# A decoder layer on one core: another order of the five products of a feed-forward chunk, and three smaller edits behind it

## The chip, the core and the metric

The kernel runs on one core of a Trainium2 chip. Five engines work side by side, each through its own list of instructions in order: TensorE (PE in the profile; PEld is its weight load), VectorE (DVE), ScalarE (ACT), GpSimd (POOL) and SyncE (SP), which here only issues DMAs. They wait for each other through semaphores. The metric is the time of one execution in microseconds (us).

## What is computed

One layer over 1056 tokens (1024 of a prompt, 8 x 4 being decoded), width 1024, inner width 2816. The part that matters is the feed-forward block and the embedding step behind it; the mixing step ahead of them is untouched.

```python
f = _rms(x, n_ffn_pre)
f = (jax.nn.silu(f @ w_gate) * (f @ w_up)) @ w_down
x = x + _rms(f, n_ffn_post)
x = x + jax.nn.sigmoid(x @ w_ple_gate) * (p @ w_ple)
```

All of it is float32. The kernel makes a float32 product out of three faster ones: every operand is split into a high part (a cast on ScalarE, L185) and a low part (the difference on VectorE, L186), and the product of the two low parts is left out.

## The kernel before

**Products with seven multiplications.** The three large matrix products of this part are done as 2 x 2 block products with seven block multiplications in place of eight. Their operands are sums and differences of blocks, named S1 to S4 for the weights and T1 to T4 for the tokens, beside plain blocks B11 to B22. A multiplication is named after the weights it uses: P1, P2 and P4 use plain weights, S1 to S4 sums.

**The channel chunks.** Gate and up projection go through 22 chunks `c` of 128 inner columns (`chunk(c)`). P1 and P2 of all chunks are made earlier by `ahead`, and their results are parked in device memory. `part_load` (L1159) fetches them as a tile `p` that holds p1 and c11. What is left for a chunk are five products on TensorE: P4, S2, S4, S3, S1 (P4 reads the weight tile `w`, the S products read `sh` and `sl`; the tokens are `fh`). A product is 24 matmuls of 128 x 264 into one PSUM pair (two banks, `b` in the profile); there are four pairs. VectorE empties a pair with a sum (`add`, L1127): p1 += S2, then u4 = p1 + S4, u3 = p1 + S3, c21 = u3 + P4, and S1 (p5 in the code) is added to u3 and u4. The chunk ends with c21 times silu(c11), silu of u4 on ScalarE (L1202), u3 times u4, and in `chunk_put` (L1069 and L1064) the differences t1, t2, t4 and the one for T3, which go to device memory as the operands `xd` of the down projection. One chunk of each two stores five such tiles, the other two.

**Weights of the chunks.** `need` walks a list of items. For each chunk the list has `half` (the weights of P4, one tile `w`, cast from a quarter of the raw up weights) and `sums` (GpSimd makes the four sums in place over the raw tiles `wr` and `a`, L1099, and then four tiles `sh`, `sl` are split from them). GpSimd's first sum overwrites what `w` is split from, so it comes after that split. All split weights share one ring of 2 x W_PAIRS = 8 tiles: five for a chunk, so the weights of two chunks on take tiles that products of the current chunk free.

**The down projection** follows the chunks: five groups of columns for each of P1, P2, S2, S3, P4, S1, S4, with four pairs filled in turn (`down`), and the tokens `xo` loaded from `xd` (L1323) and split. Its weight sums are made during the chunks by GpSimd: `down_sums`, eleven slabs of four operations `ds` (L1303), each slab loaded by SyncE and stored to `dd`. During the first part of the down stage `gate_sums` makes the sums for the embedding gate (`ws`, L1099; loads L1267, stores to `gd` L1277), one step at every call of `gates_on`.

**The last stage** multiplies by w_ple_gate: eight half products with W1, then S4, S1, S2, S3 and P4 with W2, each followed by `ple_end` (sigmoid, L1483, times the embedding product `pp`, plus the residual `xm`, then the store of the output). The two embedding weights WE are taken from the ring of eight and stay in use until the end; `need(..., 3)` prepares the weights three items ahead. The norm between (`rstd_steps`, with a tile `hl`, and then `o`, `x` and `eh` rows) runs on VectorE and ScalarE at the same time.

**What sets the order.** The program is written in one order, and a scheduler places the instructions of each engine from it; instructions marked with `keep_in_program_order` stay where they are. At run time nothing is reordered on VectorE, ScalarE, GpSimd or SyncE: an instruction that waits holds all that stands behind it.

Of the kernel before, what the change touches and what calls it, by code (L numbers as in the profile page):

```python
# [12 lines left out]
AF = mybir.ActivationFunctionType  # L13
ALU = mybir.AluOpType
# [22 lines left out]
FFC = 22  # L37
# [3 lines left out]
QN = T // 4  # L41
# [28 lines left out]
def trunk_kernel(  # L70
# [68 lines left out]
    def pair():  # L139
        return psum[0].tile([P, 2, 512], F32, tag="p", name=nm("b"))  # L140
# [7 lines left out]
    def row(s="r"):  # L148
        return tmp(HN, s).rearrange("p (i n) -> p i n", n=QN)
# [61 lines left out]
    def w_split(j, home=None):  # L211
        if j >= len(plan) or j in pairs:
            return
        w_load(j)
        shape = plan[j][1]
        hi, lo = (home(shape, F32R) if home else w_tile(shape, s) for s in ("wh", "wl"))
        split(hi, lo, raws[j])
        pairs[j] = (hi, lo)
# [37 lines left out]
    WG = []  # L256
# [51 lines left out]
    def need(k, ahead=LOOK):  # L308

        for i in range(len(made), max(k + 1, min(k + ahead + 1, until[0]))):  # L310
            kind, js = ITEMS[i]
            if kind == "loaded":
                made[i] = w_tile([P, 2, 512], "wf")
                queue(nc.sync.dma_start(made[i].bitcast(F32), js[0]))
                continue
            for j in plans(kind, js):
                w_load(j)
            if kind == "direct":
                w_split(js[0])
                made[i] = pairs[js[0]]  # L320
            elif kind == "half":
                t = w_tile([P, KC, P], "w2")
                made[i] = t[:, 0:4, :], t[:, 4:8, :]
                split(*made[i], raws[js[0]][:, js[1] : js[1] + 4, :])
            else:
                made[i] = w_sums(*(raws[j] for j in js))
            for kind, js in ITEMS[i + 1 : i + 3]:
                for j in plans(kind, js):
                    w_load(j)
        return made[k]  # L330
# [707 lines left out]
    def operand(key, i=None):  # L1038
        while (key not in fx) if i is None else ((key, i) not in ready):
            step(chains[0])  # L1040
        return fx[key]
# [24 lines left out]
    def chunk_put(c, h0, h1):  # L1066

        def sub(out, a, b):
            ve.tensor_tensor(out, a, b, op=ALU.subtract)  # L1069

        pair_, slot = c // SLAB, c % SLAB
        if slot == 0:
            stage("B11", pair_, h0)
            t1 = row("t1")
            sub(t1, h1, h0)
            stage("T1", pair_, t1)
            evens[:] = t1, h1
            return
        t1, b12 = evens
        stage("B21", pair_, h0)  # L1080
        stage("B22", pair_, h1)
        t2, t4 = row("t2"), row("t4")
        sub(t2, h1, t1)
        stage("T2", pair_, t2)
        sub(t4, h0, t2)
        stage("T4", pair_, t4)
        sub(b12, h1, b12)
        stage("T3", pair_, b12)
# [23 lines left out]
    def ops4(w, x, i):  # L1112

        at = [(k // 2, 2 * (k % 2) + i) for k in range(4)]
        return [
            (w[0][:, k, :], w[1][:, k, :], x[0][t][:, j, :], x[1][t][:, j, :]) for k, (t, j) in enumerate(at)
        ]

    def product(w, x, onto=None):

        ps = pair()[:, :, :QN] if onto is None else onto
        for i in range(2):
            gemm(ps[:, i, :], ops4(w, x, i), onto=onto is not None)
        return ps

    def add(out, a, b, op=ALU.add):
        ve.tensor_tensor(out, a, b, op=op)  # L1127
# [28 lines left out]
    def part_load(c):  # L1156
        if c < FFC:
            parts[c] = act_tile([P, 2, 2, QN], s="p")
            nc.sync.dma_start(parts[c], p_d[c])  # L1159

    def seven(w, sums, p1, x):

        p4 = product(need(w), x("T4"))
        s = need(sums)
        add(p1, p1, product(s["S2"], x("T2")))
        u4 = row("u4")
        add(u4, p1, product(s["S4"], x("B22")))
        u3 = row("u3")
        add(u3, p1, product(s["S3"], x("T3")))
        c21 = row("c21")  # L1170
        add(c21, u3, p4)
        yield c21
        p5 = product(s["S1"], x("T1"))
        add(u3, u3, p5)
        yield u3
        add(u4, u4, p5)
        yield u4

    sums = []

    def sums_on(n=1):
        if not sums:
            sums.append(down_sums())
        for _ in range(n):
            next(sums[0], None)

    def chunk(c):

        part_load(c + 1)
        p = parts.pop(c)  # L1190
        p1, c11 = p[:, 0], p[:, 1]
        ins = se.activation(c11, c11, AF.Silu)
        if c == 0:
            tc.keep_in_program_order(ins)
        made7 = seven(*WG[c], p1, operand)
        c21 = next(made7)
        add(c21, c21, c11, ALU.mult)
        sums_on()
        c22 = next(made7)
        c12 = next(made7)  # L1200
        sums_on(1 + c % 2)
        se.activation(c12, c12, AF.Silu)  # L1202
        add(c22, c22, c12, ALU.mult)
        chunk_put(c, c21, c22)
        if c == FFC - 2:
            sums_on(4 * NSLAB)

    os_ = [[None] * 2 for _ in range(2)]
    x2 = [[None] * 2 for _ in range(2)]
# [166 lines left out]

    share[0] = 0.5
    queued[:] = [None]
    gates = (x for n in range(4) for x in gate_sums(n))

    def gates_on(e, j):
        if j == 3:
            next(gates, None)

    def squares_end(o, b):
# [88 lines left out]
    def ple_end(gate, xm, pp, m, b, pieces=WHOLE, onto=None):  # L1474

        sg = row("sg")
        for at in pieces:
            at = (slice(None), *at)
            g = gate[at]
            if onto is not None:  # L1480
                add(onto[at], onto[at], g)
                g = onto[at]
            se.activation(sg[at], g, AF.Sigmoid)  # L1483
        for at in pieces:
            at = (slice(None), *at)
            add(sg[at], sg[at], pp[at], ALU.mult)
            add(sg[at], sg[at], xm[at])
            dst = by_row(y_o[:, m, HN * b : HN * (b + 1)])
            nc.sync.dma_start(dst[at], sg[at])
# [62 lines left out]
    on()  # L1552
    u2 = {}
    for a, _ in PAIRS:
        ps = product(need(W1[a][0], 3), e7["B11"])
        if a in (5, 1):
            both = two_rows("p1")
        u2[a] = both[a in (7, 3)]
        se.copy(u2[a], ps)
        xm = x2_row(a, 0)  # L1560
        pp = embed(WE[a // 4], a, 0)
        on()
        product(need(W1[a][1], 3), e7["B21"], ps)
        ple_end(ps, xm, pp, a, 0)
        on()

    c12, p5 = {}, {}
    for k in LATE:
        for g in range(2):
            for i in range(2):  # L1570
                a, b = PAIRS[2 * g + i]
                w = need(W2[k, a], 3)
                if k != "P4":
                    w = [w[:, h].rearrange("p (k n) -> p k n", n=P) for h in range(2)]
                last = k == LATE[-1] and g == i == 1
                key = {"S4": "B22", "P4": "T4"}.get(k, "T" + k[1])
                ps = product(w, e7[key])
                if k == "S4":
                    if i == 0:
                        both = two_rows("c12")  # L1580
                    c12[a] = both[i]
                    se.copy(c12[a], ps)
                elif k == "S1":
                    if i == 0:
                        both = two_rows("p5")
                    p5[a] = both[i]
                    se.copy(p5[a], ps)
                    add(c12[a], c12[a], ps)
                elif k == "S2":
                    xm = x2_row(a, 1)  # L1590
                    pp = embed(WE[a // 4], a, 1)
                    add(u2[a], u2[a], ps)
                    ple_end(u2[a], xm, pp, a, 1, onto=c12[a])
                elif k == "S3":
                    xm = x2_row(b, 1)
                    pp = embed(WE[b // 4], b, 1)
                    add(u2[a], u2[a], ps)
                    ple_end(u2[a], xm, pp, b, 1, onto=p5[a])
                else:
                    xm = x2_row(b, 0)  # L1600
                    if last:
                        pp = late_pp
                    else:
                        pp = embed(WE[b // 4], b, 0)
                    if g == 1 and i == 0:
                        late_pp = embed(WE[PAIRS[3][1] // 4], PAIRS[3][1], 0)
                    ple_end(ps, xm, pp, b, 0, onto=u2[a], pieces=PIECES if last else WHOLE)
                on()
# [90 lines left out]
```

## Time and profile before

| what | us |
|---|---|
| three runs of the kernel before | 1070.43, 1070.84, 1075.89 |
| median | 1070.84 |
| the profiled execution | 1073.98 |
| its span in the profile | 1072.2 |
| channel chunks, about | 395 to 728 |
| down projection, about | 728 to 958 |
| last stage, about | 958 to 1072 |

The span is the time from the first to the last instruction of the profiled execution; the time of the execution is 1.8 us longer. Rows of the profile name an instruction by its line in the kernel, the tiles it writes and reads (`u<-p,b`), their shapes and how often it occurs. In a group of instructions the first number behind the bar is the busy time in us and the second the mean of one in ns; behind the next bar stands the idle time of the engine ahead of them and what ended it. A busy time near 100% of TensorE says that it had work, not that it ran at full speed; the granted clock is a column of its own.

### The profile page before, as it was taken

To read this page: it belongs to the slowest core of one execution; us is meant where nothing else is said; L and a number is where in the kernel's file an instruction comes from. 1 tells how busy PE (TensorE), PEld (TensorE's weight loads), DVE (VectorE), ACT (ScalarE), POOL (GpSimd) and SP (SyncE) were. 2 spreads that over 40 slices of the span, in tenths; PEclk is the share of its full clock that TensorE was granted. 3 is DMA by queue.
4 is the path that set the end of the run, shared out by engine and by line. 5 is a ranking of instruction groups with operands and counts; after the bars stand their busy time and mean duration, and the time that the engine had idled before them with its cause. 6 is when DMAs were issued, how large, how long until landed. Compare 5 with 4: busy or idle time off the path is not lost.

```text
span 1072.2 us, 20467 instructions
## 1 busy us (share of the span) xinstructions
PE 1046.4 (98%) x8175; PEld 1028.4 (96%) x8175; DVE 774.9 (72%) x1078; ACT 472.7 (44%) x872; POOL 272.7 (25%) x213
## 2 busy tenths in 40 slices
PE   9999999999999999899999999998999999999997
PEld 8999988899999999899999999998999999999997
DVE  6866378977798827769768787786457667979765
ACT  7522277765677642221222222332454445444421
POOL 1045023200000038567566654312022200000000
PEclk9999999999999999999999999999999999999999
DMA  8121311362889757877777775457687887747763
GB/s 300 60 73 40 101 57 41 124 230 80 285 294 316 245 204 249 298 273 256 248 274 264 260 249 192 144 182 245 199 288 249 318 269 243 229 166 254 230 231 117
DMA packets 115903, 224.56 MB, mean 209 GB/s; under 512 B 9668, under 2 KB 60132, under 8 KB 115808
## 3 DMA queue, kind: packets, MB, share of 16 engines
q1 hardware_dynamic: 114480, 221.49, 61.4%
q10 hardware_dynamic: 1328, 1.77, 0.5%
q8 instruction: 64, 1.05, 0.4%
q14 instruction: 31, 0.25, 0.1%
HBM read 156.15 MB, written 67.07 MB: 208 GB/s over the span
## 4 chain that ended last, share of the span: by engine, by line
PE 42%; POOL 4%; DVE 4%; issue 4%; DMA 3%; ACT 1%; SPq 0%; POOLq 0%; DVEq 0%; ACTq 0%
PE b L135 42%; POOL ds L1303 2%; POOL wr L1099 1%; POOL a L1099 1%; DMA p<-pd 1%; DVE u L1127 1%; DMA wr<-in_w_dn_dram 0%; DVE w L186 0%; DMA xo<-xd 0%; DMA xd<-u 0%; DVE t L1069 0%; DVE o L1251 0%; DVE x L1127 0%; DVE sg L1127 0%; DMA dd<-ds 0%
## 5 line engine op out<-in xcount | busy, mean ns | idle before, releaser
L135 PE MATMUL b<-fh,sh 128*128 128x264 f32 x1408 | 258.8, 285 | 8.6 <-DVE p L1127 8.6
L135 PE MATMUL b<-xo,wh 128*128 128x264 f32 x1232 | 225.3, 285 | 3.9 <-DVE u L1127 3.9
L135 PEld LDWEIGHTS b<-fh,sh 128*128 128x128 f32 x1408 | 219.2, 190 | 9.8 <-DVE p L1127 9.8
L135 PE MATMUL b<-fh,sl 128*128 128x264 f32 x704 | 200.3, 285 | 0.0
L135 PEld LDWEIGHTS b<-xo,wh 128*128 128x128 f32 x1232 | 191.9, 190 | 4.2 <-issue 4.1
L135 PE MATMUL b<-xo,wl 128*128 128x264 f32 x616 | 175.5, 285 | 0.0
L186 DVE TENSOR_TENSOR wl<-wr,wh 128x1024 fp32r<-128x1024 f32 (+1 forms) x106 | 128.2, 1213 | 51.7 <-ACT wh L185 49.9
L185 ACT CAST wh<-wr 128x1024 fp32r<-128x1024 f32 (+1 forms) x106 | 105.3, 997 | 99.2 <-PE b L135 85.4
L135 PEld LDWEIGHTS b<-fh,sl 128*128 128x128 f32 x704 | 133.7, 190 | 0.0
L135 PE MATMUL b<-fh,wh 128*128 128x264 f32 x704 | 127.7, 283 | 1.5 <-ACT st L1145 1.5
L135 PEld LDWEIGHTS b<-xo,wl 128*128 128x128 f32 x616 | 117.0, 190 | 0.0
L135 PE MATMUL b<-h,wh 128*128 128x352 f32 x480 | 113.0, 326 | 0.9 <-ACT h L466 0.9
L135 PEld LDWEIGHTS b<-fh,wh 128*128 128x128 f32 x704 | 108.5, 188 | 2.1 <-ACT st L1145 2.1
L1099 POOL TENSOR_TENSOR a<-a 128x512 f32<-128x512 f32 x22 | 28.3, 1288 | 279.8 <-DVE w L186 245.2
L135 PE MATMUL b<-fh,wl 128*128 128x264 f32 x352 | 99.2, 282 | 0.0
L186 DVE TENSOR_TENSOR xo<-xo 128x528 fp32r<-128x528 f32 x77 | 62.1, 824 | 35.4 <-ACT xo L185 35.2
L185 ACT CAST sh<-wr 128x1024 fp32r<-128x1024 f32 x22 | 23.1, 1048 | 144.9 <-POOL wr L1099 144.9
L135 PEld LDWEIGHTS b<-h,wh 128*128 128x128 f32 x480 | 83.6, 190 | 2.0 <-ACT h L466 1.2
L185 ACT CAST xo<-xo 128x528 fp32r<-128x528 f32 x77 | 47.7, 632 | 65.3 <-DMA xo<-xd 60.4
L186 DVE TENSOR_TENSOR sl<-wr,sh 128x1024 fp32r<-128x1024 f32 x22 | 26.9, 1225 | 65.6 <-ACT sh L185 65.6
L135 PE MATMUL b<-h,wl 128*128 128x352 f32 x240 | 73.9, 325 | 0.0
L135 PE MATMUL b<-fh,w 128*128 128x264 f32 x528 | 67.8, 284 | 1.4 <-DVE u L1127 0.8
(186 smaller groups left out, 2006.2 us busy)
## 6 DMA issues: line engine op xcount, KB each, us to landing
wr<-in_w_gu_dram SPq DMA_DIRECT2D x58, 512.0 KB, 4.8
xo<-xd SPq DMA_DIRECT2D x77, 264.0 KB, 6.8
pd<-st SPq DMA_DIRECT2D x44, 264.0 KB, 4.5
p<-pd SPq DMA_DIRECT2D x22, 528.0 KB, 5.1
a<-in_w_gu_dram SPq DMA_DIRECT2D x22, 512.0 KB, 4.5
ds<-in_w_dn_dram SPq DMA_DIRECT2D x22, 512.0 KB, 5.2
dd<-ds SPq DMA_DIRECT2D x22, 512.0 KB, 3.9
wr<-dd SPq DMA_DIRECT2D x20, 512.0 KB, 7.1
```

The costliest lines, as they stand in the source:

```text
L135: ins = te.matmul(*args, **kw)
L185: fix(se.copy(hi, src))
L186: fix(ve.tensor_tensor(lo, src, hi.bitcast(F32), op=ALU.subtract))
L1099: ge.tensor_tensor(out, a, b, op=op)
L1127: ve.tensor_tensor(out, a, b, op=op)
L1303: ge.tensor_tensor(out, a, b, op=op)
```

## The change

Five things are edited:

1. A chunk's products run in the order S2, S4, S3, P4, S1, where P4 was the first. The generator `seven` is written out in `chunk`.
2. A chunk's end (c21 times c11, the silu, u3 times u4, `chunk_put`) is written behind the first two products and sums of the next chunk (`chunk_end`), and the load of the next chunk's part behind that. The last chunk ends itself.
3. The embedding weights WE take large tiles of the pool that also holds operands (`act_tile`) instead of the ring, and the last stage looks 6 and 5 items ahead instead of 3.
4. The gate sums start at the third call of `gates_on` with j == 3 instead of the first.
5. The very last product writes its two halves to two PSUM tiles, so that `ple_end` can treat the first half by itself.

```diff
-                w_split(js[0])
+                w_split(js[0], act_tile if i in WE.values() else None)
...
+    unput = []
+
+    def chunk_end():
+        while unput:
+            c, c11, c21, c22, c12 = unput.pop()
+            add(c21, c21, c11, ALU.mult)
+            se.activation(c12, c12, AF.Silu)
+            add(c22, c22, c12, ALU.mult)
+            chunk_put(c, c21, c22)
+
     def chunk(c):
-        part_load(c + 1)
         p = parts.pop(c)
         p1, c11 = p[:, 0], p[:, 1]
         ins = se.activation(c11, c11, AF.Silu)
...
-        made7 = seven(*WG[c], p1, operand)
-        c21 = next(made7)
-        add(c21, c21, c11, ALU.mult)
+        half, sums = WG[c]
+        s = need(sums)
+        add(p1, p1, product(s["S2"], operand("T2")))
+        u4 = row("u4")
+        add(u4, p1, product(s["S4"], operand("B22")))
+        chunk_end()
+        part_load(c + 1)
         sums_on()
-        c22 = next(made7)
-        c12 = next(made7)
+        u3 = row("u3")
+        add(u3, p1, product(s["S3"], operand("T3")))
+        c21 = row("c21")
+        add(c21, u3, product(need(half), operand("T4")))
+        p5 = product(s["S1"], operand("T1"))
+        add(u3, u3, p5)
+        add(u4, u4, p5)
         sums_on(1 + c % 2)
-        se.activation(c12, c12, AF.Silu)
-        add(c22, c22, c12, ALU.mult)
-        chunk_put(c, c21, c22)
+        unput.append((c, c11, c21, u3, u4))
         if c == FFC - 2:
             sums_on(4 * NSLAB)
+        if c == FFC - 1:
+            chunk_end()
...
     def gates_on(e, j):
-        if j == 3:
+        gates_at[0] += j == 3
+        if j == 3 and gates_at[0] > 2:
             next(gates, None)
...
-        ps = product(need(W1[a][0], 3), e7["B11"])
+        ps = product(need(W1[a][0], 6), e7["B11"])
...
-                w = need(W2[k, a], 3)
+                w = need(W2[k, a], 5)
...
-                ps = product(w, e7[key])
+                if last:
+                    ps = [pair()[:, h, :QN] for h in range(2)]
+                    for h in range(2):
+                        gemm(ps[h], ops4(w, e7[key], h))
+                else:
+                    ps = product(w, e7[key])
```

How this moves instructions shows in each engine's list. First VectorE, in the chunks, where chunk 1 ends and chunk 2 begins. `sl_4902` and `sl_4866` are low parts of S weights of chunk 3; `p` with `b` empties S2 of chunk 2; u times u and the L1069 rows are the end of chunk 1. Before:

```order
L186 TENSOR_TENSOR sl_4902<-wr_4734,sh_4901 128x1024
L1127 TENSOR_TENSOR u_4964<-u_4964,u_4937 128x528
L1069 TENSOR_TENSOR t_5036<-u_4964,t_4860 128x528
L1069 TENSOR_TENSOR u_4789<-u_4964,u_4789 128x528
L1069 TENSOR_TENSOR t_5037<-c_4991,t_5036 128x528
L1127 TENSOR_TENSOR p_4864<-p_4864,b_5094 128x528
L186 TENSOR_TENSOR sl_4906<-a_4695,sh_4905 128x1024
```

And after the change:

```order
L186 TENSOR_TENSOR sl_4866<-wr_4707,sh_4865 128x1024
L1127 TENSOR_TENSOR p_4937<-p_4937,b_5049 128x528
L1127 TENSOR_TENSOR u_4940<-u_4940,u_4901 128x528
L1069 TENSOR_TENSOR u_4773<-u_4940,u_4773 128x528
L1127 TENSOR_TENSOR u_5075<-p_4937,b_5076 128x528
L1069 TENSOR_TENSOR t_5109<-u_4940,t_4933 128x528
L186 TENSOR_TENSOR sl_4870<-a_4693,sh_4869 128x1024
L1069 TENSOR_TENSOR t_5110<-c_4967,t_5109 128x528
```

The row `p` has moved ahead of the end of the chunk before, and the end is spread over the sums that follow.

Second GpSimd, at the weight sums of chunk 7 (`a` and `wr`) and a slab `ds` of the down projection. Before:

```order
L1099 TENSOR_TENSOR a_5403<-a_5403 128x512
L1099 TENSOR_TENSOR a_5403<-wr_5442,a_5403 128x512
L1099 TENSOR_TENSOR wr_5442<-a_5403,wr_5442 128x512
L1099 TENSOR_TENSOR wr_5442<-wr_5442 128x512
L1303 TENSOR_TENSOR ds_5910<-ds_5910 128x512
L1303 TENSOR_TENSOR ds_5910<-ds_5908,ds_5910 128x512
L1303 TENSOR_TENSOR ds_5908<-ds_5910,ds_5908 128x512
L1303 TENSOR_TENSOR ds_5908<-ds_5908 128x512
```

And after:

```order
L1099 TENSOR_TENSOR a_5383<-a_5383 128x512
L1099 TENSOR_TENSOR a_5383<-wr_5397,a_5383 128x512
L1303 TENSOR_TENSOR ds_5909<-ds_5909 128x512
L1099 TENSOR_TENSOR wr_5397<-a_5383,wr_5397 128x512
L1303 TENSOR_TENSOR ds_5909<-ds_5907,ds_5909 128x512
L1099 TENSOR_TENSOR wr_5397<-wr_5397 128x512
L1303 TENSOR_TENSOR ds_5907<-ds_5909,ds_5907 128x512
L1303 TENSOR_TENSOR ds_5907<-ds_5907 128x512
```

Two rows of the slab now stand between the weight sums. In the whole list this is so, with one to three rows, at 8 of the 11 slabs; before, it was at the first slab alone.

Third VectorE again, where the last chunk (21) ends and the down projection's tokens `xo` are split; `u`, `c` with `b` empty its pairs. Before:

```order
L1127 TENSOR_TENSOR u_8454<-p_8189,b_8455 128x528
L1127 TENSOR_TENSOR c_8481<-u_8454,b_8370 128x528
L186 TENSOR_TENSOR xo_8602<-xo_8602 128x2x264
L1127 TENSOR_TENSOR c_8481<-c_8481,p_8189 128x528
L186 TENSOR_TENSOR xo_8606<-xo_8606 128x2x264
L1127 TENSOR_TENSOR u_8454<-u_8454,b_8484 128x528
L1127 TENSOR_TENSOR u_8427<-u_8427,b_8484 128x528
```

And after:

```order
L1127 TENSOR_TENSOR u_8429<-p_8255,b_8430 128x528
L186 TENSOR_TENSOR xo_8602<-xo_8602 128x2x264
L186 TENSOR_TENSOR xo_8654<-xo_8654 128x2x264
L186 TENSOR_TENSOR xo_8658<-xo_8658 128x2x264
L186 TENSOR_TENSOR wl_8356<-wr_8176,wh_8355 128x1024
L1127 TENSOR_TENSOR c_8456<-u_8429,b_8457 128x528
L1127 TENSOR_TENSOR c_8456<-c_8456,p_8255 128x528
L1127 TENSOR_TENSOR u_8429<-u_8429,b_8483 128x528
```

The sum `c`, which was ahead of the xo rows, now stands behind three of them.

More of the change, by code (lines that the diff above doesn't have):

```diff
@@ L1159, in part_load @@
             nc.sync.dma_start(parts[c], p_d[c])
[L1161 to L1177, printed above, removed]
     sums = []
@@ L1378, in trunk_kernel @@
     queued[:] = [None]
+    gates_at = [0]
     gates = (x for n in range(4) for x in gate_sums(n))
     def gates_on(e, j):
-        if j == 3:
+        gates_at[0] += j == 3
+        if j == 3 and gates_at[0] > 2:
             next(gates, None)
@@ L1478, in ple_end @@
             at = (slice(None), *at)
-            g = gate[at]
+            g = gate[at] if pieces is WHOLE else gate[at[1].start][:, at[2]].unsqueeze(1)
             if onto is not None:
@@ L1562, in trunk_kernel @@
         on()
-        product(need(W1[a][1], 3), e7["B21"], ps)
+        product(need(W1[a][1], 6), e7["B21"], ps)
         ple_end(ps, xm, pp, a, 0)
```

## Prediction

> **What bounds the kernel now.** I read the page first. One engine is nearly always busy:
>
> ```profile
> span 1072.2 us, 20467 instructions
> PE 1046.4 (98%) x8175; PEld 1028.4 (96%) x8175; DVE 774.9 (72%) x1078; ACT 472.7 (44%) x872; POOL 272.7 (25%) x213
> ```
>
> The change removes no matmul, so all it can win is time in which TensorE stands still or runs slowly, and the work behind its last matmul. The waits view of TensorE says for whom it stands still (total, times, longest):
>
> ```profile
> PE b L135 <- DVE p L1127: 8.6, 6, 3.1
> PE b L135 <- DVE u L1127: 4.8, 2, 3.9
> PE b L135 <- DVE w L186: 1.8, 1, 1.8
> ```
>
> The timeline of TensorE gives the places (start, duration; in brackets the idle time before):
>
> ```profile
> 439.60 0.53 PE L135 MATMUL b<-fh,sh 128*128 128x264 f32 x2 [3.07 <-DVE p L1127]
> 564.69 0.52 PE L135 MATMUL b<-fh,sh 128*128 128x264 f32 x2 [1.93 <-DVE p L1127]
> 736.61 0.52 PE L135 MATMUL b<-xo,wh 128*128 128x264 f32 x2 [3.94 <-DVE u L1127]
> 983.61 2.94 PE L135 MATMUL b<-eh,w 128*128 128x264 f32 x22 [1.81 <-DVE w L186]
> ```
>
> The six waits for p lie in the channel chunks. Of the two for u, one (4.8 - 3.94 = 0.9) lies there too, the other at the start of the down stage; the wait for w is in the last stage. The table by stretches (length, busy time of each engine, granted clock, DMA) shows what some of them cost again:
>
> ```profile
> 430.00:450.00 20.00, 16.93 (x128) 16.72 (x127) 15.52 (x16) 6.53 (x9) 13.00 (x9) 0.91 0.82 278
> 565.00:570.00 5.00, 5.00 (x31) 5.00 (x30) 4.93 (x7) 0.00 (x0) 3.39 (x3) 0.66 0.83 288
> 730.00:740.00 10.00, 6.06 (x39) 5.88 (x38) 9.19 (x9) 5.03 (x7) 4.52 (x3) 0.85 0.26 87
> ```
>
> The lost clock is 20 x 0.09 = 1.8 us, 5 x 0.34 = 1.7 us and 10 x 0.15 = 1.5 us. Together: 8.6 + 0.9 waiting and 3.5 of clock in the chunks, 3.9 + 1.5 at the down stage, 1.8 in the last stage: 20.2 us.
>
> [...]
>
> **Chunks: why TensorE waits.** One product (24 matmuls) takes 2.88 us, from the starts of two successive ones:
>
> ```profile
> 458.55 3.04 PE L135 MATMUL b<-fh,w 128*128 128x264 f32 x24
> 461.43 0.40 PE L135 MATMUL b<-fh,sh 128*128 128x264 f32 x2
> ```
>
> Five products make a chunk, 14.4 us. There are four PSUM pairs, so a product waits for the sum that empties the product four places ahead. The worst wait, by VectorE's timeline:
>
> ```profile
> 433.11 1.80 DVE L1127 TENSOR_TENSOR u<-u,u 128x528 f32<-128x528 f32 x1
> 434.95 1.68 DVE L1069 TENSOR_TENSOR t<-u,t 128x528 f32<-128x528 f32 x1
> 436.55 1.76 DVE L1069 TENSOR_TENSOR u<-u,u 128x528 f32<-128x528 f32 x1
> 438.24 0.70 DVE L1069 TENSOR_TENSOR t<-c,t 128x528 f32<-128x528 f32 x1
> 438.86 0.69 DVE L1127 TENSOR_TENSOR p<-p,b 128x528 f32<-128x528 f32 x1
> ```
>
> Row p empties S2. In front of it stands the previous chunk's end: u times u, then three differences t, u, t, 5.75 us together. The change puts p in front of these (the first pair of order pieces). Then p could have run from 433.1 and ended near 434, before TensorE ran dry at 436.5 (439.60 - 3.07). In the other five places the same rows stand ahead of p. So the 8.6 + 0.9 and the 3.5 of clock go in their present form: **-13.0**. Counting the moved end at nothing rests on VectorE having room: it was busy 240 of the 315 us of this stage.
>
> ```profile
> 430.00:745.00 315.00, 301.62 (x2451) 300.02 (x2450) 240.23 (x278) 84.80 (x114) 165.44 (x113) 0.98 0.71 238
> ```
>
> **What is late next.** With P4 in fourth place, the tile of its weights is free only 2.88 us before a chunk ends, and the weights w of two chunks on are split into it. Behind that split stand GpSimd's four sums, then a cast sh and a difference sl, then S2 of that chunk. Their rows (busy, mean ns of one | idle before):
>
> ```profile
> L185 ACT CAST w<-a 128x512 fp32r<-128x512 f32 x20 | 12.3, 617 | 28.3 <-PE b L135 28.3
> L186 DVE TENSOR_TENSOR w<-a,w 128x512 fp32r<-128x512 f32 x12 | 11.1, 923 | 1.7 <-ACT w L185 1.7
> L1099 POOL TENSOR_TENSOR wr<-a,wr 128x512 f32<-128x512 f32 x15 | 22.9, 1524 | 1.1
> L1099 POOL TENSOR_TENSOR a<-a 128x512 f32<-128x512 f32 x15 | 19.3, 1287 | 63.1 <-DVE w L186 37.2 <-ACT st L1149 11.4 <-DMA xd<-u 9.7
> L185 ACT CAST sh<-wr 128x1024 fp32r<-128x1024 f32 x21 | 22.0, 1049 | 141.4 <-POOL wr L1099 141.4
> L186 DVE TENSOR_TENSOR sl<-wr,sh 128x1024 fp32r<-128x1024 f32 x13 | 15.9, 1225 | 39.5 <-ACT sh L185 39.5
> L1303 POOL TENSOR_TENSOR ds<-ds 128x512 f32<-128x512 f32 x22 | 35.6, 1620 | 15.7 <-DMA ds<-in_w_dn_dram 8.3 <-issue 6.5
> ```
>
> The chain is 0.6 + 0.9 + four sums of about 1.4 + 1.0 + 1.2 = 9.3 us. From the end of P4(c) to the start of S2(c+2) lie six products, 17.3 us: 8.0 to spare, where before the split could begin after S4(c), eight products ahead (23.0, 13.7 to spare). GpSimd also makes the down stage's sums ds, four to a slab; in the new order 8 of 11 slabs stand between the weight sums (second pair of pieces). A whole slab is 4 x 1.6 = 6.5 us, which fits by 1.5. But a ds row also waits for its load, issued by SyncE behind the previous slab's stores and one of the t stores; such a load takes 5.2 us (section 6 of the page):
>
> ```profile
> ds<-in_w_dn_dram SPq DMA_DIRECT2D x22, 512.0 KB, 5.2
> ```
>
> At the slab of the second piece I work out: two ds rows (3.2) and about half a load, 2.6 to 5.2, stand in the chain: 9.3 + 3.2 + 5.2 = 17.7 against 17.3, and VectorE and ScalarE take their rows in order, which may add one row of about 1. So a slab costs nothing to 1.4. Ends: 0 (nothing waits) and 8 x 1.4 = 11.2, with clock on top. I take 0.55 a slab, below the middle since five of the eight hold a single weight sum between their ds rows: **+4.5**. The rest of the new order (part loads issued later on SyncE) I cost at nothing, since on SyncE p's load stands a chunk ahead of its use; if that cover fails it is one more wait of the 1 to 2 us kind.
>
> **Start of the down stage.** The last chunk's sums are late because of rows that wait for loads, and GpSimd's gate sums slow them:
>
> ```profile
> 729.35 1.26 ACT L185 CAST xo<-xo 128x528 fp32r<-128x528 f32 x2 [5.54 <-DMA xo<-xd]
> 731.78 1.78 DVE L1127 TENSOR_TENSOR c<-c,p 128x528 f32<-128x528 f32 x1
> 733.48 1.76 DVE L186 TENSOR_TENSOR xo<-xo 128x528 fp32r<-128x528 f32 x1
> 735.16 1.30 DVE L1127 TENSOR_TENSOR u<-u,b 128x528 f32<-128x528 f32 x2
> ```
>
> The same kind of row takes 0.7 elsewhere (row 438.24), so c and xo lose about 1.1 each, and a third, xo at 730.0, as much: 3.2 us. The gate loads and sums now begin two steps later, past this point, and no longer stand between the xo loads on SyncE. Against it, the third pair of pieces shows three xo rows, not one, ahead of c. Ends: all 5.4 won, or nothing if xo lands as late. I keep 1.0 of waiting, too short to cost clock by most of the waits above: **-4.4**.
>
> **Last stage.** Embedding weights leave the ring of eight, so four more tiles are free; all eight W1 splits now stand ahead of the norm's rows (in the new order the last w is in front of hl), so the wait at 983.61 goes: **-1.8**. What it adds, a longer row of splits ahead of hl, is 0.7 us against one wl less of 1.2. Ends: 0 and -1.8; four act tiles less for the loads could give the 1.8 back.
>
> **End.** The last matmul ends at 1066.64 and the last row of VectorE at 1069.29:
>
> ```profile
> 1066.66 0.83 DVE L1127 TENSOR_TENSOR p<-p,b 128x264 f32<-128x264 f32 x3 [2.85 <-PE b L135]
> 1067.13 0.83 ACT L1483 ACTIVATE sg<-p 128x264 f32<-128x264 f32 x3 [4.89 <-DVE p L1127]
> 1068.68 0.28 DVE L1127 TENSOR_TENSOR sg<-sg,b 128x132 f32<-128x132 f32 x1
> 1069.00 0.29 DVE L1127 TENSOR_TENSOR sg<-sg,xm 128x132 f32<-128x132 f32 x1
> ```
>
> With two tiles the first half is finished under the second half's 12 matmuls. Left are two sums of 0.25, two products and two sums of 0.28: 1.7 instead of 2.65: **-0.95**. Ends: 0 and -1.2. The second tile needs a pair emptied long before.
>
> **The sum.** -13.0 + 4.5 - 4.4 - 1.8 - 0.95 = -15.65. The profiled execution took 1073.98 us: 1058.3. That execution lies 3.1 above the median of the runs, 1070.84; I do not subtract this, since the waits that are left, not those removed, should then set the time. **Forecast 1058.**
>
> **Rivals.**
> - *All waits go.* GpSimd and the loads keep up: 1058.3 - 4.5 - 1.0 = 1053. For it: GpSimd is busy 165 of 315 us. Against: its ds rows waited 8.3 us for loads already.
> - *Every slab costs its 1.4, and two clock losses come back:* 1058.3 + 6.7 + 3.5 = 1068.5.
> - *The change does not do what it says:* p is no longer behind the chunk's end, but sl still stands ahead of it and waits for GpSimd (39.5 us idle before it above), so the six waits stay and only the other places win: 1073.98 - 4.4 - 1.8 - 0.95 = 1067. [...] Against it: at the worst wait VectorE was past sl and at u by 433.11.
> - *Slower:* the weight sums become the bound. If a slab stands in the chain whole and its load is waited out, 9.3 + 6.5 + 5.2 - 17.3 = 3.7 us are lost in each of the eight, 30 us: 1083. It is slower than before from 2.9 a slab. Against: each wait gives GpSimd the same time to catch up.
>
> **How the numbers follow.** Forecast 0.60 (its own range 1054 to 1063), all gone 0.17, slabs in full 0.10, waits stay 0.06, slower 0.07. A measurement of this kernel can tell about 0.5% from no change, 5.4 us: faster is below 1065.5, slower above 1076.2. Faster: 0.77 and 0.03 of the third case's lower end, 0.80; same 0.13; slower 0.07. The range 1051 to 1068 takes in the first four cases but for the third's upper half.
>
> **What would show it.** In the profile after: no wait for p (L1127) among the chunks; if waits are left there, they end on sl (L186), or on a sum right behind it, in the chunks with ds rows (until about 620 us) and before a first product S2, not a last S1. No clock loss between 430 and 745, or one. A wait below 2 us before the first xo matmuls; none for w in the last stage; under 2 us from the last matmul to VectorE's last row. I am wrong if TensorE's waits in the chunks sum to over 9 us, or if the down stage starts as late as now.

## The result, and the profile after

| | us, median | range of the runs | ratio to before, 95% interval |
|---|---|---|---|
| before (same chip) | 1070.63 | 1068.24 to 1075.89 | |
| after the change | 1125.11 | 1123.58 to 1129.15 | 1.0508 [1.046, 1.0555] |

The changed kernel is 5% slower. The profiled execution took 1124.59 us. The page of the changed kernel starts:

```profile
span 1122.6 us, 20465 instructions
PE 1057.8 (94%) x8175; PEld 1038.2 (92%) x8175; DVE 743.9 (66%) x1078; ACT 471.9 (42%) x872; POOL 263.2 (23%) x213
```

The matmuls are the same number; TensorE is busy 94% of a longer span instead of 98%. Its waits (total, times, longest):

```profile
PE b L135 <- DVE p L1127: 41.8, 12, 6.0
PE b L135 <- ACT p L1561: 5.7, 1, 5.7
PE b L135 <- DVE u L1127: 4.5, 4, 2.9
PE b L135 <- DVE c L1127: 2.0, 1, 2.0
```

The wait for p, which was to vanish, went from 8.6 to 41.8 us. Some of the places, by the timeline of TensorE of the changed kernel:

```profile
510.65 0.81 PE L135 MATMUL b<-fh,sh 128*128 128x264 f32 x2 [4.91 <-DVE p L1127]
547.28 0.81 PE L135 MATMUL b<-fh,sh 128*128 128x264 f32 x2 [5.13 <-DVE p L1127]
605.91 0.81 PE L135 MATMUL b<-fh,sh 128*128 128x264 f32 x2 [6.03 <-DVE p L1127]
641.52 0.51 PE L135 MATMUL b<-fh,sh 128*128 128x264 f32 x2 [3.96 <-DVE p L1127]
...
782.81 0.48 PE L135 MATMUL b<-xo,wh 128*128 128x264 f32 x2 [1.99 <-DVE c L1127]
...
1030.58 7.96 PE L135 MATMUL b<-eh,w 128*128 128x264 f32 x48 [5.71 <-ACT p L1561]
```

By the first matmul of chunk 0 and the first ones that use `xo` and `eh`, the span divides so (us):

| | before | after | difference |
|---|---|---|---|
| ahead of the chunks | 395.3 | 396.2 | +0.9 |
| chunks, to the first matmul with xo | 332.9 | 380.4 | +47.5 |
| down projection, to the first with eh | 229.9 | 228.2 | -1.7 |
| last stage, to the end of the span | 114.1 | 117.8 | +3.7 |

So the loss is made in the chunks. By the rows of TensorE and the record of the clock, TensorE stands still there for 45.2 us instead of 9.6, which is 35.6 of the 47.5, and works at half clock for 27.6 us instead of 6.8, which costs about 10 more. The row at 605.91 shows its kind; the timelines of VectorE, GpSimd and ScalarE of the changed kernel ahead of it:

```profile
588.55 0.69 DVE L186 TENSOR_TENSOR w<-a,w 128x512 fp32r<-128x512 f32 x1
...
592.48 1.28 POOL L1303 TENSOR_TENSOR ds<-ds 128x512 f32<-128x512 f32 x1 [12.44 <-DMA ds<-in_w_dn_dram]
593.84 2.66 POOL L1303 TENSOR_TENSOR ds<-ds,ds 128x512 f32<-128x512 f32 x2
596.46 1.28 POOL L1099 TENSOR_TENSOR a<-a 128x512 f32<-128x512 f32 x1
597.70 1.29 POOL L1303 TENSOR_TENSOR ds<-ds 128x512 f32<-128x512 f32 x1
...
601.64 1.26 POOL L1099 TENSOR_TENSOR wr<-wr 128x512 f32<-128x512 f32 x1
...
602.94 1.04 ACT L185 CAST sh<-wr 128x1024 fp32r<-128x1024 f32 x1 [19.82 <-POOL wr L1099]
...
604.02 1.23 DVE L186 TENSOR_TENSOR sl<-wr,sh 128x1024 fp32r<-128x1024 f32 x1 [12.93 <-ACT sh L185]
605.16 0.70 DVE L1127 TENSOR_TENSOR p<-p,b 128x528 f32<-128x528 f32 x1
```

w is split at 589.2, yet GpSimd begins its sum for that chunk at 596.5: a ds row stands ahead that waits for its load until 592.5; it and two more take 3.9 us, and the fourth stands between the sums. Then sh, sl and p, one behind the other, and TensorE starts 0.05 us after p. The row p uses nothing that sl makes; it stands behind sl on VectorE.

Without any ds row the same loop looks so (changed kernel, timelines of ScalarE, VectorE and GpSimd):

```profile
676.76 0.70 DVE L1127 TENSOR_TENSOR p<-p,b 128x528 f32<-128x528 f32 x1
...
677.82 0.62 ACT L185 CAST w<-a 128x512 fp32r<-128x512 f32 x1 [0.84 <-PE b L135]
...
681.33 0.68 DVE L186 TENSOR_TENSOR w<-a,w 128x512 fp32r<-128x512 f32 x1
...
682.10 1.70 POOL L1099 TENSOR_TENSOR a<-a 128x512 f32<-128x512 f32 x1 [8.21 <-DVE w L186]
...
686.61 1.29 POOL L1099 TENSOR_TENSOR wr<-wr 128x512 f32<-128x512 f32 x1
...
687.93 1.05 ACT L185 CAST sh<-wr 128x1024 fp32r<-128x1024 f32 x1 [3.78 <-POOL wr L1099]
...
689.01 1.23 DVE L186 TENSOR_TENSOR sl<-wr,sh 128x1024 fp32r<-128x1024 f32 x1 [5.15 <-ACT sh L185]
690.16 0.70 DVE L1127 TENSOR_TENSOR u<-u,u 128x528 f32<-128x528 f32 x1
690.77 0.70 DVE L1127 TENSOR_TENSOR p<-p,b 128x528 f32<-128x528 f32 x1
```

From one p to the next it takes 690.77 - 676.76 = 14.0 us, although no ds row is in between; the next two p rows (705.85 and 720.22) follow after 15.1 and 14.4. TensorE's five products take 14.4. The kernel before has the same rows in another order:

```profile
650.63 0.62 ACT L185 CAST w<-a 128x512 fp32r<-128x512 f32 x1 [1.16 <-PE b L135]
...
651.21 0.70 DVE L1127 TENSOR_TENSOR p<-p,b 128x528 f32<-128x528 f32 x1
...
663.09 0.70 DVE L1127 TENSOR_TENSOR p<-p,b 128x528 f32<-128x528 f32 x1
```

There 11.9 us lie from p to p, and w is cast at 650.63, when S4, the third product, is done. The product that needs the pair which p empties is S1 of the next chunk (the waits for p at 439.60 and 564.69, shown in the prediction, lie ahead of that last product too). It starts six products, 17.3 us, after the end of S4, and p ends at 663.79, so about 4 us are to spare. In the changed kernel w is cast when P4, the fourth, is done, and only five products, 14.4 us, are left.

### The profile page after: what moved, and what is told of

It reads as the page before. It is cut to its first block, busy times and chain, and to the rows that moved or that the text cites. A ratio compares the mean times of both kernels' runs of the same rounds, so it can differ in the third digit from the quotient of the medians.

```text
span 1122.6 us, 20465 instructions
## 1 busy us (share of the span) xinstructions
PE 1057.8 (94%) x8175; PEld 1038.2 (92%) x8175; DVE 743.9 (66%) x1078; ACT 471.9 (42%) x872; POOL 263.2 (23%) x213
## 5 line engine op out<-in xcount | busy, mean ns | idle before, releaser
L135 PE MATMUL b<-fh,sh 128*128 128x264 f32 x1408 | 269.3, 292 | 45.6 <-DVE p L1127 41.8
L135 PEld LDWEIGHTS b<-fh,sh 128*128 128x128 f32 x1408 | 227.1, 196 | 48.9 <-DVE p L1127 44.3
L135 PE MATMUL b<-fh,sl 128*128 128x264 f32 x704 | 204.5, 291 | 0.0
L185 ACT CAST wh<-wr 128x1024 fp32r<-128x1024 f32 (+1 forms) x104 | 102.9, 995 | 95.6 <-PE b L135 85.9
L135 PEld LDWEIGHTS b<-fh,sl 128*128 128x128 f32 x704 | 138.2, 196 | 0.0
L1099 POOL TENSOR_TENSOR a<-a 128x512 f32<-128x512 f32 x22 | 34.4, 1564 | 312.7 <-DVE w L186 292.8
```

Source lines behind the costliest of these rows:

```text
L135: ins = te.matmul(*args, **kw)
L185: fix(se.copy(hi, src))
L1099: ge.tensor_tensor(out, a, b, op=op)
```

## The experiments

The theory that I tested (loop theory, A and F in the expectations): p, w, the four weight sums, sh, sl and the next p make a loop through three engines that the new order leaves no slack in, and ds rows, or waits for loads, lengthen the chunk by what they bring into it. Its rivals: the deferred end does it by the loads it delays (C and D), SyncE's queue does it wherever GpSimd works (G), or parts 3 to 5 do it (B).

**Which part: four pieces of the change alone, on the kernel before.** `chunks_only` is parts 1 and 2, `rest_only` parts 3 to 5, `order_only` part 1, `defer_only` part 2. The last two differ from the changed kernel's `chunk` in this (and have parts 3 to 5 undone). In `order_only` the part load keeps the later place that it has in the changed kernel, so it is not quite part 1 alone. The groups of runs below were taken on different chips, where the kernel before had medians from 1070.6 to 1075.1 us; differences of a few us between groups are therefore read with the ratios and their intervals.

```diff
 order_only
-        chunk_end()
         part_load(c + 1)
...
         unput.append((c, c11, c21, u3, u4))
+        chunk_end()

 defer_only
+        p4 = product(need(half), operand("T4"))
         s = need(sums)
...
-        add(c21, u3, product(need(half), operand("T4")))
+        add(c21, u3, p4)
```

> Parts 1 and 2 alone (order of the products, deferred chunk end); gate sums, embedding weights, lookahead and last product as before. Theory A (the loss is made in the chunks, where the row p on VectorE stands behind sl, whose GpSimd sums start only after P4): the chunks lose what they lose in the changed kernel, TensorE waits for p over 35 us and the half clock with them; about 1112 to 1118. Rival B (the embedding weights in the large tiles delay loads and rows in the chunks as well): the chunks run as I had forecast, about 1062 to 1072.

> Parts 3, 4 and 5 alone; the chunks as before. Theory A: the waits of the chunks are those of before (8.6 us for p), the last stage shows the long wait for the copy p of an embedding product (5.7 us, with clock about 8), the down stage starts with a shorter wait; 1072 to 1080. Rival B: the chunks lose here too, over 1100. If the last stage's wait came only from the chunks running late, it is absent here and the time is 1064 to 1069.

> Part 1 alone: products in the order S2, S4, S3, P4, S1, but each chunk ends itself, as before; parts 3 to 5 undone. Theory A (the order moves the split of w behind P4, and so GpSimd's sums, sl and p): most of the loss is here, 1100 to 1125, TensorE waits for p in a dozen places. Rival C (the deferred end does it: the stores and the part load issued later on SyncE hold up the loads of ds): near before, 1060 to 1075.

> Part 2 alone: the chunk's end put behind the first sums of the next chunk, the products in the order of before (P4 first); parts 3 to 5 undone. Theory A: w is split after S4 as before, p no longer stands behind the chunk's end, so some or all of the 8.6 us and the clock go: 1058 to 1070. Rival C: 1095 to 1120, with waits on p behind sl as in the changed kernel.

| | us, median | ratio to before, 95% interval | waits for p; u |
|---|---|---|---|
| chunks_only | 1125.41 | 1.0494 [1.0439, 1.0548] | 35.0; 7.9 |
| rest_only | 1077.61 | 1.0041 [1.0017, 1.0066] | 8.3; 2.0 |
| order_only | 1145.95 | 1.0673 [1.0621, 1.0726] | 55.6; 10.8 |
| defer_only | 1089.46 | 1.0144 [1.0101, 1.0187] | 5.5; 18.9 |

Parts 1 and 2 alone are as slow as the whole change, which settles B. The order with the late part load is slower still, so the deferred end helps the new order, by 20 us. Both came out above their expected ranges (1112 to 1118 and 1100 to 1125). But the deferred end alone costs 17 us as well, which the loop theory did not expect: the waits for p do shrink, as intended, and waits for u take their place. The largest, by the timelines of ScalarE, VectorE and TensorE of `defer_only`:

```profile
490.45 0.64 ACT L1183 ACTIVATE p<-p 128x528 f32<-128x528 f32 x1 [10.69 <-issue]
491.00 0.60 ACT L185 CAST w<-a 128x512 fp32r<-128x512 f32 x1
...
491.63 0.69 DVE L186 TENSOR_TENSOR w<-a,w 128x512 fp32r<-128x512 f32 x1 [8.40 <-ACT w L185]
492.24 0.70 DVE L1127 TENSOR_TENSOR u<-p,b 128x528 f32<-128x528 f32 x1
...
493.08 4.85 PE L135 MATMUL b<-fh,w 128*128 128x264 f32 x24 [6.60 <-DVE u L1127]
```

ScalarE stands at the silu of a part p that has not landed (its load was issued at 483.1, behind the deferred stores, and landed at 490.3); w's cast stands behind the silu, w's difference behind that on VectorE, and behind it the sum u that empties the pair which P4 waits for. So there are two mechanisms, not one.

**GpSimd's slab sums.** `no_ds` leaves the operations out, `ds_small` does 16 of 512 columns, and `ds_behind` does all of them, pinned behind the four weight sums:

```diff
 no_ds
-                ge.tensor_tensor(out, a, b, op=op)

 ds_small
+                ge.tensor_tensor(out[:, 0:16], a[:, 0:16], b[:, 0:16], op=op)

 ds_behind
         quarter_sums(a1, a2)
+        if pinned_sums[0]:
+            nth[0] += 1
+            sums_on(2 + nth[0] % 2)
...
+                tc.keep_in_program_order(ge.tensor_tensor(out, a, b, op=op))
...
-        sums_on()
-        sums_on(1 + c % 2)
```

> The changed kernel without GpSimd's 44 operations ds in the chunks; their loads and stores stay, so the down stage multiplies by weights that are not summed. Theory A (the chain from the end of P4 over the split of w, four GpSimd sums, sh and sl to the row p has 14.4 us until S1 of the next chunk needs p's PSUM pair, and the ds rows with their waits for loads lie in it): the chain without them is about 0.7 + 0.7 + 5.8 + 1.0 + 1.2 + 0.7 = 10 us, so the waits for p in the chunks fall from 41.8 to under 12 us; 1070 to 1085. Rival D (the part load, issued later, lets the silu of p hold the cast of w on ScalarE, whatever GpSimd does): over 1105.

> The changed kernel with each operation ds over 16 of 512 columns; the rest of the sums is left out, all loads, stores and waits stay. If GpSimd's time is what costs (in the loop, and beside VectorE's rows): as without ds, 1073 to 1085. If the waits cost that ds brings into the queues of GpSimd and SyncE (a ds row that waits for its load, a store behind which the part load stands): over 1095, with idle time of GpSimd that ends on the loads of ds.

> The changed kernel with GpSimd's operations ds pinned behind the four weight sums of a chunk, two and three by turns, so that none stands between the split of w and the last of its sums; as many of them as before, with the same loads and stores. Theory F (the rows p, w, the four sums, sh, sl and the next p make a loop through three engines that takes about 14.1 us with no ds in it, TensorE's five products 14.4; what lies in the loop beside them lengthens the chunk by its whole time): with the ds rows in GpSimd's idle 8 us of each loop the waits for p fall from 41.8 to under 15 us; 1076 to 1090. Rival G (the ds rows cost because their loads and stores hold up SyncE's queue, wherever GpSimd does them): over 1105.

| | us, median | ratio to before, 95% interval | waits for p |
|---|---|---|---|
| no_ds | 1076.39 | 1.0027 [1.0004, 1.0049] | 8.5 |
| ds_small | 1104.11 | 1.0291 [1.0252, 1.033] | 29.1 |
| ds_behind | 1102.67 | 1.0267 [1.0232, 1.0302] | 26.6 |

The 44 operations cost 1125.1 - 1076.4 = 48.7 us, nearly the whole loss. The place is the same: without them the chunks take 331.8 us in the profile, with them 380.4. (The kernel before, with all its ds rows, takes 332.9; what they cost there no run shows.) Their time alone is 1125.1 - 1104.1 = 21 of it; 28 us stay in `ds_small` with 10 us of GpSimd time (44 operations of 0.23). I put these down to what waits in the queues: in `ds_small` too, at four slabs ds rows stand ahead of weight sums for 2.3 to 2.8 us, after w is split, until their own load lands. Both theories about ds were half right: `ds_small` came out where the waits were expected to cost (over 1095), `ds_behind` between the ranges of F (1076 to 1090) and G (over 1105). Taking the rows out of the chain brought 22 us, not the 35 to 49 expected. One reason is seen in the groups of VectorE between 430 and 640 us (busy, mean ns), first of `no_ds`:

```profile
L1127 DVE TENSOR_TENSOR u<-u,u 128x528 f32<-128x528 f32 x14 | 9.8, 702 | 0.0
```

and of `ds_behind`, where GpSimd's ds rows now run while VectorE has this row between sl and p:

```profile
L1135 DVE TENSOR_TENSOR u<-u,u 128x528 f32<-128x528 f32 x13 | 21.2, 1629 | 0.0
```

0.93 us more in each loop: its p rows start at 500.26, 516.91 and 532.03, 16.7 and 15.1 us apart, although no ds row lies between the sums. The row p<-p,b, with one input in PSUM, keeps its length: 692 ns in `ds_behind` against 697 in `no_ds`. The rows of the kernel before between 395 and 790 us show the same: where a GpSimd row runs beside them for over 90% of their time, u<-u,u (L1127) takes 1800 ns (7 rows) and p<-p,b 693 (6), and where next to none does, 703 (15) and 697 (16).

**The ring and the place of sl.** `ring9` gives the split weights nine tiles (and nine row tiles instead of eleven for room), `rows9` takes the row tiles alone, `ring9_behind` adds the pinned ds. `late_split` writes the splits of sh and sl a chunk later:

```diff
 ring9
-ROWS = 11
+ROWS = 9
...
-        return wpool.tile(shape, F32R, tag="wp", bufs=2 * W_PAIRS, name=nm(s))
+        return wpool.tile(shape, F32R, tag="wp", bufs=9, name=nm(s))

 late_split
-        s = need(sums)
+        raw = need(sums)
+        s = splits.pop(c) if c in splits else s_split(*raw)
...
         add(u4, p1, product(s["S4"], operand("B22")))
+        if c + 1 < FFC:
+            splits[c + 1] = s_split(*need(WG[c + 1][1], 0))
```

> The changed kernel with a ring of nine split weight tiles in place of eight (the room comes from the row tiles, 9 in place of 11). w of two chunks on then takes a tile that S4 frees, not P4: 5.8 us more for the chain. Theory A: most of the waits for p go, what is left are whole slabs with a long wait for a load; 1070 to 1090. Rival D: over 1105. If two row tiles less cost much by themselves, new waits of VectorE for row tiles show and the time says nothing.

> The changed kernel with nine row tiles in place of eleven, nothing else. If the two row tiles cost what the ring of nine showed outside the loop (waits of 5.6 and 5.1 us, clock with them, and row tiles missing in the chunks): 1136 to 1150, and the ninth weight tile was worth some 25 us or more. If they cost nothing: 1122 to 1128, and the ninth tile was worth the 12 us that the ring of nine gained.

> ds_behind with the ring of nine tiles (and nine row tiles): ds out of the loop and w split after S4, not P4. Loop theory: w may start 5.8 us earlier, the loop is no longer as long as five products, the chunks lose under 10 us; with the wait in the last stage 1075 to 1090. If GpSimd's time beside VectorE is a cost of its own: within 8 us of ds_behind, 1095 to 1105.

> The changed kernel with the splits sh and sl of a chunk's four S weights written behind the second sum of the chunk before it, instead of a chunk earlier; w and GpSimd's sums are made as early as before. No sl stands ahead of p any longer unless its sums are done. Theory A: the waits for p go to under 5 us in the chunks; 1065 to 1085 in all, since the wait in the last stage stays. Rival D: the silu of p, late by its load, still holds rows on ScalarE: waits of 3 to 6 us in several chunks, over 1095.

The loop theory expected 1070 to 1090 us of `ring9`, 1065 to 1085 of `late_split` and 1075 to 1090 of `ring9_behind`; none came out so. `ring9` took 1113.13 us (1.036 [1.0317, 1.0403]), `rows9` 1122.29 (1.0462 [1.0434, 1.0489]), `ring9_behind` 1126.05 (1.0491 [1.0451, 1.053]), `late_split` 1124.73 (1.0477 [1.0424, 1.0524]). With the ninth tile no wait for p is left in the chunks, but twelve for u (18.9 us) and one of 5.6 us for a row st of ScalarE at their start come in; its gain is 9 to 12 us, since `rows9` shows the row tiles to cost nothing. That sum hides two effects. In the profiles the chunks take 350.9 us in `ring9` against 378.9 in `rows9`, 28 less, as far as the later start does not help them; but the stretch ahead of the chunks takes 413.9 against 395.2, with waits of 5.1 and 5.6 us and half-clock stretches that `rows9` does not have. So the time over 1105, which rival D had forecast, does not come from D's cause, and the larger ring bears out the loop theory in the chunks. With ds pinned on top the chunks take 362.6 us, more than in `ring9`, and the stretch ahead of them is as long as there (411.6); why the two do not add up stays open. `late_split` came out in rival D's range (over 1095): sl no longer holds p, but the waits for p stay, and the chunks take 379.5 us against 380.4. Its timelines of SyncE and ScalarE show another holder, the silu of D:

```profile
524.19 0.32 SPq L1317 DMA_DIRECT2D dd<-ds  x1
...
526.34 0.41 SPq L1163 DMA_DIRECT2D p<-pd  x1
...
532.12 0.64 ACT L1188 ACTIVATE p<-p 128x528 f32<-128x528 f32 x1 [20.86 <-DMA p<-pd]
532.67 0.60 ACT L185 CAST w<-a 128x512 fp32r<-128x512 f32 x1
```

The part load stands on SyncE behind a store of slab sums, which waits for GpSimd, whose rows wait for w; and w waits behind the silu for the part. The loop closes through SyncE too. Moving sl alone therefore gains nothing.

**The part load.** `part_early` and `defer_early` issue it at the chunk's start, in the changed kernel and in `defer_only`. `ds_behind_early` and `ds_behind_silu` are `ds_behind` with part 3 undone, the one with the early load, the other with the silu written in `chunk_end`.

```diff
+        part_load(c + 1)
         p = parts.pop(c)
...
         chunk_end()
-        part_load(c + 1)
```

> The changed kernel with the load of the next chunk's part at the start of the chunk, where the kernel before has it, instead of behind the deferred end. Theory A: a small gain, 1105 to 1123, since the chain over GpSimd stays as long; the waits on u and those where the cast of w stands behind the silu of p go. Rival D: the late part load is most of the loss; 1065 to 1085.

> The deferred end alone (order of before, parts 3 to 5 undone), with the part load at the start of the chunk as before. If the late part load made the loss of the deferred end (the silu of p held the cast of w on ScalarE, 6.6, 4.7 and 3.8 us): those waits go, 1062 to 1075. If not, within 5 us of the deferred end alone, 1084 to 1094.

> ds_behind with the load of the part at the start of the chunk, and the embedding weights and lookahead as in the kernel before (part 3 undone). Theory F: the long wait for the copy p in the last stage goes (5.7 us and its clock, some 7 to 9 us), a wait of 1.8 us for w comes back; 1065 to 1080. It is the version that could beat both kernels. Rival G: over 1095.

> ds_behind with part 3 undone and the silu of p written in the deferred end, in front of the product that needs it, instead of at the start of the chunk; the part load stays behind the deferred end. If the silu that waits for its load and stands ahead of the cast of w on ScalarE still costs in ds_behind, this is 3 to 10 us faster than with the silu at the start; 1065 to 1078. If it does not, no difference that can be told from ds_behind with part 3 undone.

`part_early` took 1119.79 us (1.0427 [1.0385, 1.0468]), 5 less than the changed kernel, as the loop theory had it; the intervals just overlap, and in the profiles the chunks take 374.5 us against 380.4. `defer_early` took 1075.28 (1.0021 [0.9997, 1.0046]): 14 of the 17 us that the deferred end alone cost were the late load. `ds_behind_early` took 1112.29 (1.0356 [1.0326, 1.0386]) and `ds_behind_silu` 1100.26 (1.0241 [1.0212, 1.027]); both missed their ranges (1065 to 1080 and 1065 to 1078), and neither is a version to keep. `ds_behind_silu` waits for p as long as `ds_behind` (27.1 us against 26.6) and its chunks take 361.1 us against 359.7, so the place of the silu gains nothing there that can be told. In the former the part load again stands on SyncE behind stores, and the silu holds w's cast (477.17 where P4 ended at 468.8). Why it is slower than `ds_behind` in sum stays open.

**The small parts.** `no_we` is the changed kernel without part 3; `gates_last` is parts 4 and 5 on the kernel before.

```diff
 no_we
-                w_split(js[0], act_tile if i in WE.values() else None)
+                w_split(js[0])
...
-                w = need(W2[k, a], 5)
+                w = need(W2[k, a], 3)
```

> The changed kernel with part 3 undone: embedding weights from the ring of eight, lookahead 3. Theory: the copy p of an embedding product no longer waits for a large tile that a row x of VectorE frees (5.7 us and two half windows of the clock, 3.4 us), the wait of 1.8 us for w comes back: 7 us faster than the changed kernel, 1116 to 1120. If the time is within 2 us of 1125, something else in the last stage takes the place of the wait.

> Parts 4 and 5 alone on the kernel before: gate sums from the third call on, last product in two tiles. The start of the down stage loses 1 to 2 us in place of 3.9 and its clock, the end is 0.8 us shorter, the chunks and the last stage are those of before: 1068 to 1072 where before is 1072 to 1075, a ratio of 0.994 to 0.998.

`no_we` took 1117.47 us (1.0409 [1.037, 1.0448]), 7.6 less than the changed kernel, and its last stage takes 112.5 us in the profile against 117.8: the long wait there belongs to part 3. VectorE and ScalarE of the changed kernel there:

```profile
1028.58 1.26 DVE L1127 TENSOR_TENSOR x<-x,o 128x1056 f32<-128x1056 f32 x1
...
1029.92 0.60 ACT L1561 COPY p<-b 128x528 f32<-128x528 f32 x1 [7.73 <-DVE x L1127]
```

The copy of a product into a new large tile waits until a row x of VectorE has let go of one: the four tiles that the embedding weights took from the large pool. `gates_last` took 1070.86 (0.9995 [0.9967, 1.0022]): the wait at the start of the down stage is gone in its trace, but its chunks waited 11.5 us for p. The ratio, expected at 0.994 to 0.998, shows no difference that can be told.

**A version that is faster than both.** `defer_best` keeps the order of before, defers the chunk's end, loads the part at the chunk's start, pins the silu of p behind the cast of w, and has parts 4 and 5:

```diff
+                w_cast[0] = cast[0].ins.name
...
         s = need(sums)
+        ins = se.activation(c11, c11, AF.Silu)
+        tc.add_manual_dep(ins.ins, w_cast[0], NOSYNC, reason="silu behind the cast of w")
         add(p1, p1, product(s["S2"], operand("T2")))
```

> The order of before, the deferred end, the part load at the start of the chunk, the silu of p pinned behind the cast of w on ScalarE, and parts 4 and 5. If the silu that waits for the part holds the cast of w and so VectorE's sums: the waits for u in the chunks (3.3 and 1.9 us) go, p no longer stands behind the chunk's end, 1058 to 1068, faster than both kernels. If not: 1070 to 1077, no faster than before.

It took 1057.61 us, 0.9855 [0.9831, 0.9879] of before, just under the expected 1058 to 1068. TensorE's waits in its chunks, by the waits view, and the granted clock there, by the table by stretches (the number behind the five busy times):

```profile
PE b L135 <- DVE p L1131: 2.0, 2, 1.1
PE b L135 <- DVE u L1131: 1.5, 3, 0.6
...
395.00:730.00 335.00, 331.34 (x2736) 330.21 (x2737) 279.15 (x301) 93.76 (x126) 201.24 (x132) 1.00 0.73 251
```

Its chunks take 322.5 us, the down stage 226.9, the last stage 112.5: 10.4, 3.0 and 1.6 less than before. `defer_early`, which has neither the pin of the silu nor parts 4 and 5, takes 336.2 us in the chunks, so the deferred end and the early load alone do not win them; no run has the pin without parts 4 and 5.

## Why the prediction was wrong, step by step

- **p behind the chunk's end (-13.0).** The rows named were the cause of these waits as far as `defer_best` shows: there most of the chunk's end stands behind p too, and with the part load early and the silu behind w's cast the chunks are 10.4 us shorter and lose no clock. In the changed kernel none of it is seen, since p waits behind sl instead; even without ds rows, in `no_ds`, 8.5 us of waits for p stay.
- **What is late next (+4.5).** This is the step that failed. I gave the chain from the end of P4(c) six products, 17.3 us, with its deadline at the first use of the weights, S2(c+2). Its real deadline is one product earlier: sl of c+2 stands ahead of p(c+1) on VectorE, and S1(c+1) needs p's pair, five products, 14.4 us. And I took 9.3 us for the chain, without the queue ahead of w on VectorE (677.8 to 681.3) and without the row u times u and p themselves at its end: from the end of P4 at 677.8 to p's end at 691.5 it is 13.7. So 0.7 us were to spare, not 8.0. With that, much of what a slab brings in is lost: 48.7 us over eleven slabs, 4.4 each with the clock, where I had 0 to 1.4 and chose 0.55. A slab's four rows take 5.8 us of GpSimd, and its load's wait, which I had at 2.6 to 5.2 us inside the chain, was 2.1 to 3.2 at the slabs where it held the weight sums after w's split. Of the signs that I named, the waits did end on a sum right behind sl, but ahead of S1 and not of S2. Nor does a product always wait for the one four places ahead: in the kernel before S1 takes the pair of S2, three places ahead.
- **The part load "at nothing".** I wrote that its failure would be one wait of 1 to 2 us. Alone (`defer_only` against `defer_early`) it costs 14 us, in waits of up to 6.6; in the changed kernel about 5.
- **Down stage (-4.4).** The waits there are 0.9, 2.0 and 0.3, not 1.0: 3.2 in place of 3.9, and no clock lost; later in the stage a wait of 1.0 for a split of xo is new. The stage is 1.7 us shorter.
- **Last stage (-1.8).** The wait for w did go, and the price that I had seen at its other end, that four large tiles less could give the gain back, came out at 5.7 us of waiting and two half stretches of the clock. Of their 6.8 us TensorE works 4.3, so they cost 2.1.
- **End (-0.95).** From the last matmul's end to VectorE's last row it is 1.9 us instead of 2.65: -0.75, by these rows of the changed kernel's TensorE and VectorE:

```profile
1114.69 3.04 PE L135 MATMUL b<-eh,w 128*128 128x264 f32 x24
...
1119.15 0.49 DVE L1127 TENSOR_TENSOR sg<-sg,xm 128x132 f32<-128x132 f32 x2
```

- **The rivals.** The one called slower had the mechanism, weight sums as the bound, and the rival that p would stay behind sl had the place. I held them apart and gave both little. Together they are what happened: because p stands behind sl, the sums bound the chunk at once and not only from 2.9 us a slab. The argument against the former, that each wait lets GpSimd catch up, fails in a loop: its next sums wait for a w that waits for the same p.

What stays open: how the 28 us that do not come from GpSimd's time divide between ds rows that wait for loads and SyncE's stores that hold the part, and why the pinned ds and the ninth tile do not add up.

## What to carry to other kernels

When rows are moved in front of a row that frees a buffer, ask what stands ahead of the freed row on its own queue, not only what it needs: the deadline of a producer chain is the first row queued behind its end (here p behind sl, which left 14.4 us where I had counted 17.3). Follow the chain until it closes; where it comes back to itself, compare its length with the period of the bound engine, and count in full whatever shares a queue with it (here four engines' queues and SyncE's). And moving a store behind later work moved the loads behind that store as well: in `defer_only` the part load, behind the deferred stores, was issued at 483.1 and landed at 490.3, and the late load cost 14 us.

## What was not expected of the hardware

Between the first chunk and the last matmul the half-clock stretches in the changed kernel's record of the clock last 3.41 us, and three of the eight twice that, 6.83. Their starts (520.3, 557.9, 595.4, 615.9, 653.5, 673.9, 769.5, 1039.2 on its own time scale, on which the span starts at 11.1) lie 37.55, 37.55, 20.48, 37.55, 20.48, 95.57 and 269.65 us apart: 11, 11, 6, 11, 6, 28 and 79 times 3.413. The length of a wait alone did not tell what it cost: behind the waits of 2.75 and 2.89 us (before 473.42 and 493.86) the granted clock stayed at 1.00, while behind the 1.93 us in the kernel before (564.69) one stretch of 3.41 us at half clock follows. No run was made to show what decides it.
